# DRAM weight sums of a two-layer decoder step: first layer's along eight mixer units, second layer's along prompt attention

## The chip, the core and the metric

The program runs on one core of a Trainium2 chip. TensorE (PE) does the matmuls, VectorE (DVE), ScalarE (ACT) and GpSimd (POOL) the elementwise work, SyncE (SP) issues most transfers, and 16 DMA engines carry them. Each engine works through its own instructions in order and waits for others by semaphores. The metric is the device time of one launch in microseconds (us), the median of several runs. Float32 matmuls are made of three passes over operands that are split into a high and a low part ("h" and "l" in the names), so every weight tile that comes from DRAM is cast on ACT (high part) and subtracted on DVE or POOL (low part) before TensorE may use it.

## What is computed

One inference step of a decoder trunk with two layers, for a prompt of 1024 tokens and 8 x 8 sample tokens that share weights, width 1024, ConvGLU width 2816:

```python
mem_k_p, mem_v_p = memory_kv(mem_prompt, norm_mem, w_mem_kv)
# layer 0: mixer A, RWKV-7 time mix (12 heads of 64) beside memory attention (4 heads)
x = x + concat([o_tok, o_mem]) @ w_o[0]
x = x + conv_glu(rms_norm(x, norm_ffn[0]), state_conv[0], w_ffn_up[0], ...)
ckv, kpe = shared_latent(x, pos, ...)
# layer 1: mixer B, latent attention, 6 heads: causal for the prompt,
#          against 4096 cached tokens in pages for the samples
x = x + concat([o, o_mem]) @ w_o[1]
x = x + conv_glu(rms_norm(x, norm_ffn[1]), state_conv[1], w_ffn_up[1], ...)
y = rms_norm(x, final_norm)

def conv_glu(xn, conv_prev, w_up, conv_w, conv_b, w_down):
    u = xn @ w_up                       # (tokens, 2 * 2816): gate and val
    conv = causal_conv3(gate, conv_prev, conv_w, conv_b)
    return (silu(conv) * val) @ w_down, ...
```

The up product `xn @ w_up` is done by a Strassen-like scheme with seven products in place of eight. Some of the seven need sums of blocks of `w_up`; these sums don't depend on any activation.

## The kernel before

**The sums.** `sum_weights(l)` (L1284) makes four DRAM tensors for layer l, each 512 x 2816 in float32: `vg`, `gg`, `vgg` and `all`. It does so with DMAs alone. `move` (L1289) cuts one tensor into four transfers of 128 rows, 1408 KB each. A plain copy goes out on SP's queue, an accumulating add (`accum_op=ALU.add`) on POOL's. The source's order is: copy `vg`, copy `gg`, add to `vg`, add to `gg`, copy `vgg` from `vg`, add to `vgg`, copy `all` from `vgg`, add to `all`; four transfers each, so 32 a layer, 16 copies and 16 adds. A copy from a sum waits for the adds to it, an add for the copy before it, row block by row block. `load_up` (L1302) reads the four tensors in the ConvGLU of the same layer (the tiles `wa`); layer 0's ConvGLU begins some 1200 us after the start, layer 1's some 2700 us.

**Mixer A.** `mixer_a` (L273) runs 12 units, (half, head pair): units 0 to 5 for the first 512 prompt tokens, 6 to 11 for the rest and the samples. Three stages are woven together: the projections of unit i (`front`), the chunk-inner matrices of unit i-1 (`a_inner`) and the recurrent chain of unit i-2 (`chain`, which ends with the store `odp<-y`, L1060). Each `front` reads weight tiles of 128 x 4 x 128 (`wr<-in_w_in_a`, L207, three buffers) on SP's queue, casts them on ACT (`wh`, L210) and subtracts on POOL (`wl`, L211). `merge` takes steps from several generators by their weights; beside the first unit it takes the memory projection (`memory_kv`, loads `q<-in_w_mem_kv`), beside each later unit `sums`. `sums` is the sequence of both layers' sums, 64 steps, six a unit.

**Prompt attention.** `prompt_attention` (L1924) runs 24 units, (head, pair of query blocks), with scores of one unit beside the output of the unit before, and beside them `head_proj` (weights `w_q_b`, `w_kv_b`) and `val_proj` (weights `vr`) of the next heads. Each unit stores `odp<-ob` through two `ob` buffers. After every second head's rotary step POOL copies four small tiles (`qe<-lr`, L1787). The cached pages for the decode stage that follows are gathered on POOL's queue (`dc` and `dk`).

**What sets the order.** The code is traced in the order in which `merge` takes the steps. A scheduler then places every instruction on its engine's list by priority and by simulated readiness, so an instruction that waits for nothing can move far ahead of its place in the source. SP's and POOL's lists are the order of their DMA issues. `keep_in_program_order` ties an instruction behind the one traced just before it on the same engine.

Of the kernel before, what the change touches and what calls it, by code (L numbers as in the profile page):

```python
# [100 lines left out]
class Step:  # L101
# [171 lines left out]
    def mixer_a(s, od, qmd, kvd):  # L273
# [51 lines left out]
        def front(u):  # L325
            h, p = u
            if p == 0:
                yield from s.a_norm(h)
                yield from s.a_lora(h)
            if p == 2:  # L330
                yield from s.a_gate(h)
            ctx[u] = {}
            yield from s.a_front(p, h, ctx[u])

        def chain(u):
            h, p = u
            ctx[u]["y"] = s.t(ap, [128, 576], "y", 2)
            for g in s.groups(h):
                yield from s.a_chain(p, h, ctx[u], *g)
            yield from s.a_out(p, h, ctx.pop(u))  # L340
# [26 lines left out]
        s.mslot = (ap, "q", 512, s.QB)  # L367
        s.ended = False
        mkv = s.memory_kv(kvd, 0, ("tp", "ch", "y"))
        sums = s.seq(s.sum_weights(0), s.sum_weights(1))  # L370
        for i in range(nu):
            g = []
            if i == 1:
                for j in range(1, (len(s.prows) + 127) // 128):
                    s.load_params(j, [nc.sync])
            if i > 1:
                g.append((chain(units[i - 2]), s.PW[0] + s.PW[1] * units[i - 2][0], s.PW[2]))
            if i:
                u = units[i - 1]
                g.append((s.a_inner(u[1], u[0], ctx[u]), s.PW[3] + s.PW[4] * u[0], s.PW[5]))  # L380
            g.append((front(units[i]), 130 if units[i][1] else 220))
            if i == 0:
                g.append((mkv, 22))
            else:
                g.append((s.take(sums, 6), 6))
            s.merge(g)
        s.mslot = (ap, "xn", 584, 16)
        s.drain(last(s.seq(s.mem_attention(0, qmd, kvd, od, ("mm", "sm", "sm")), s.memory_kv(kvd, 1, ("sm", "mm", "mm")))))
# [895 lines left out]
    def sum_weights(s, l):  # L1284

        nc, W = s.nc, s.I["w_ffn_up"][l]
        S = s.wsum[l] = {z: s.t(s.dp, [512, DFF], f"ws{l}{z}", 1) for z in ("vg", "gg", "vgg", "all")}

        def move(z, src, **kw):  # L1289
            eng = nc.gpsimd if kw else nc.sync  # L1290
            for r in range(0, 512, 128):
                eng.dma_start(out=S[z][r:r + 128], in_=src[r:r + 128], **kw)
                yield

        def add(z, src):
            return move(z, src, accum_op=ALU.add, max_dma_last_dim=5632)

        g1, g2, v1, v2 = (W[r:r + 512, f:f + DFF] for f in (0, DFF) for r in (0, 512))
        yield from s.seq(move("vg", v1), move("gg", g1), add("vg", g1), add("gg", g2), move("vgg", S["vg"]),
                         add("vgg", g2), move("all", S["vgg"]), add("all", v2))  # L1300
# [623 lines left out]
    def prompt_attention(s, od):  # L1924
        s.AT = (3, 2, 1, 2, 6, 3)
        s.HN = ((8, 12, 12, 1000), (8, 12, 14, 1000))
        with s.phase("pa", dict(zip(("sc", "tp", "o", "mm"), s.AT))):
            s.hd = {h: {} for h in range(NH)}
            s.lay(*[([128, NP_], z, 2) for z in ("qs0", "qs1", "qnh", "qnl", "knh", "knl")],
                  ([128, 256], "vh", 8), ([128, 256], "vl", 8), ([128, 256], "ob", 2), ([128, 8], "sm", 4), ([128, 512], "P", s.AT[4]),  # L1930
                  ([128, 4, 256], "ptH", s.AT[5]), ([128, 4, 256], "ptL", s.AT[5]))
            s.qns = s.st([128, 6, 64], "qns", 1)
            s.drain(s.head_proj(0))
            us = [(h, Q, {}) for h in range(NH) for Q in (range(4) if h < NH - 1 else (3, 2, 1, 0))]
            pr = None
            for i in range(len(us) + 1):
                g = []
                ao = iter(())
                n = 0
                if i:  # L1940
                    h, Q, u = us[i - 1]
                    ao, n = s.attn_out(h, Q, u, od), 6 * Q + 6
                if i < len(us):
                    h, Q, u = us[i]
                    if Q == 0 and h % 2 == 0:
                        ao, n = s.seq(ao, s.val_proj(h)), n + 9
                    g.append((s.attn_scores(h, Q, u), 4 * Q + 8))
                    if Q == 0 and h + 1 < NH:
                        pr = s.head_proj(h + 1)
                    if pr is not None:  # L1950
                        k = s.HN[h % 2][Q]
                        g.append((s.take(pr, k), min(k, 40)))
                s.merge([(ao, n)] + g)


    def decode(s, od, side, xd):
# [466 lines left out]
```

## Time and profile before

| | us |
|---|---|
| median of 3 runs | 3606.49 (3594.25 to 3613.16) |
| the profiled run | 3604.49 |
| its span on the core | 3602.7 |
| TensorE busy | 3329.3 (92%) |
| VectorE busy | 2322.9 (64%) |
| ScalarE busy | 1722.7 (48%) |
| GpSimd busy | 806.1 (22%) |

The profile is one execution. Beside busy times it has the granted clock of TensorE as a share of 2.4 GHz (1.00 is the 2.4 GHz level, 0.50 the 1.2 GHz level, values between are a mix over the stretch), the busy share of the 16 DMA engines, and what each instruction waited for. A matmul at the lower level is busy for about twice the time, so busy TensorE is not the same as TensorE at its peak.

### The profile page before, as it was taken

How to read it: one execution, taken by the hardware profiler on the slowest of the kernel's cores; microseconds unless marked ns; L12 is line 12 of the kernel's file. 1: busy time of each engine (PE TensorE's matmuls, PEld its weight loads, DVE VectorE, ACT ScalarE, POOL GpSimd, SP SyncE). 2: the span in 40 equal slices, each digit the busy share in tenths (PEclk: the TensorE clock that was granted, in tenths of full speed). 3: DMA queues.
4: the chain of work that ended last, by engine and by line, in shares of the span. 5: the costliest groups of instructions: out<-in, count | busy, mean ns of one | idle time of the engine just before them, and what ended most of it. 6: DMA issues, size and time to landing. Idle time of an engine off the chain costs nothing. (4 is left out here: it accounts for less than half of the span.)

```text
span 3602.7 us, 68623 instructions
## 1 busy us (share of the span) xinstructions
PE 3329.3 (92%) x25782; PEld 2838.5 (79%) x25782; DVE 2322.9 (64%) x5353; ACT 1722.7 (48%) x3769; POOL 806.1 (22%) x1204
## 2 busy tenths in 40 slices
PE   6678789999996999999999899999999999999998
PEld 4444457777655999999999888855558999989998
DVE  4455466777653577778777547744445777787776
ACT  4333345555445454545454635533335644555444
POOL 4323213232101311113222400101102311132221
PEclk9877769999887999999999999999999999999999
DMA  7999931111314354445444310335424544545443
GB/s 223 266 246 249 242 93 39 34 44 46 93 34 164 90 164 142 144 135 160 138 141 124 93 57 30 113 111 178 150 82 120 155 141 132 145 130 148 134 141 112
DMA packets 608048, 466.90 MB, mean 130 GB/s; under 512 B 51546, under 2 KB 575598, under 8 KB 601060
## 3 DMA queue, kind: packets, MB, share of 16 engines
q1 hardware_dynamic: 583924, 359.80, 33.4%
q0 software_dynamic: 18848, 98.07, 10.7%
q10 hardware_dynamic: 4944, 4.65, 0.4%
q8 instruction: 202, 3.31, 0.4%
q14 instruction: 130, 1.06, 0.1%
HBM read 436.67 MB, written 118.03 MB: 154 GB/s over the span
## 5 line engine op out<-in xcount | busy, mean ns | idle before, releaser
L1354 PE MATMUL pmm<-xh,uh 128*128 128x272 f32 x2464 | 717.2, 291 | 5.1 <-ACT xh L1137 2.8
L1355 PE MATMUL pmm<-xl,uh 128*128 128x272 f32 x2464 | 714.0, 290 | 3.2 <-DVE xl L1138 2.9
L1356 PE MATMUL pmm<-xh,ul 128*128 128x272 f32 x2464 | 715.3, 291 | 0.4 <-DVE ul L1314 0.4
L1313 ACT CAST uh<-wa 128x512 fp32r<-128x512 f32 x610 | 378.4, 622 | 488.5 <-PE pmm L1355 306.5
L1314 DVE TENSOR_TENSOR ul<-wa,uh 128x512 fp32r<-128x512 f32 x610 | 435.5, 719 | 95.9 <-ACT uh L1313 59.6
L1354 PEld LDWEIGHTS pmm<-xh,uh 128*128 128x128 f32 x2464 | 466.8, 190 | 6.9 <-ACT xh L1137 4.3
L1355 PEld LDWEIGHTS pmm<-xl,uh 128*128 128x128 f32 x2464 | 467.8, 190 | 5.0 <-DVE xl L1138 4.5
L1356 PEld LDWEIGHTS pmm<-xh,ul 128*128 128x128 f32 x2464 | 466.7, 190 | 1.1 <-DVE ul L1314 0.9
L481 PE MATMUL pdn<-hh,wh 128*128 128x272 f32 x1248 | 360.9, 290 | 7.7 <-ACT hh L1137 3.9
L482 PE MATMUL pdn<-hl,wh 128*128 128x272 f32 x1248 | 358.4, 288 | 0.7 <-DVE hl L1138 0.7
L483 PE MATMUL pdn<-hh,wl 128*128 128x272 f32 x1248 | 357.2, 288 | 1.6 <-DVE wl L211 1.6
L210 ACT CAST wh<-wr 128x512 fp32r<-128x512 f32 (+2 forms) x363 | 200.5, 563 | 311.6 <-PE pdn L482 116.4
L1361 POOL TENSOR_TENSOR ext<-nt,nt 128x272 f32<-128x272 f32 (+2 forms) x132 | 119.0, 915 | 882.4 <-ACT uh L1313 721.4
L481 PEld LDWEIGHTS pdn<-hh,wh 128*128 128x128 f32 x1248 | 235.3, 189 | 12.9 <-ACT hh L1137 7.9
L483 PEld LDWEIGHTS pdn<-hh,wl 128*128 128x128 f32 x1248 | 235.0, 189 | 2.5 <-DVE wl L211 2.5
L482 PEld LDWEIGHTS pdn<-hl,wh 128*128 128x128 f32 x1248 | 235.2, 189 | 1.1 <-DVE hl L1138 1.1
L481 PE MATMUL pmm<-xn,wh 128*128 128x292 f32 (+2 forms) x552 | 214.6, 389 | 21.3 <-ACT wh L210 17.5
L1166 DVE TENSOR_TENSOR x<-x,pdn 128x272 f32<-128x272 f32 x288 | 125.4, 435 | 132.8 <-PE pdn L483 132.2
L483 PE MATMUL pmm<-xn,wl 128*128 128x292 f32 (+2 forms) x552 | 204.2, 371 | 1.6 <-POOL wl L211 1.4
L482 PE MATMUL pmm<-xn,wh 128*128 128x292 f32 (+2 forms) x552 | 204.9, 371 | 0.0
L211 DVE TENSOR_TENSOR wl<-wr,wh 128x512 fp32r<-128x512 f32 (+2 forms) x271 | 166.6, 624 | 47.5 <-ACT wh L210 43.7
L211 POOL TENSOR_TENSOR wl<-wr,wh 128x512 fp32r<-128x512 f32 (+1 forms) x92 | 118.3, 1289 | 238.6 <-ACT wh L210 214.0
(760 smaller groups left out, 7850.1 us busy)
## 6 DMA issues: line engine op xcount, KB each, us to landing
wa<-in_w_ffn_up SPq DMA_DIRECT2D x262, 256.0 KB
wr<-in_w_ffn_down SPq DMA_DIRECT2D x164, 256.0 KB
wr<-in_w_in_a SPq DMA_DIRECT2D x84, 256.0 KB
wr<-in_w_o SPq DMA_DIRECT2D x64, 256.0 KB
wa<-ws0vg SPq DMA_DIRECT2D x44, 256.0 KB
wa<-ws0all SPq DMA_DIRECT2D x44, 256.0 KB
wa<-ws1vg SPq DMA_DIRECT2D x44, 256.0 KB
wa<-ws1all SPq DMA_DIRECT2D x44, 256.0 KB
```

What stands on the lines that cost most here:

```text
L210: nc.scalar.copy(wh[:, :n, :m], wr[:, :n, :m])
L211: s.wl_eng.tensor_tensor(wl[:, :n, :m], wr[:, :n, :m], wh[:, :n, :m].bitcast(F32), ALU.subtract)
L481: nc.tensor.matmul(ps[:m, :n], wh[:, :m], xh[:, c0:c0 + n], start=(k == 0), stop=False)
L482: nc.tensor.matmul(ps[:m, :n], wh[:, :m], xl[:, c0:c0 + n], start=False, stop=False)
L483: nc.tensor.matmul(ps[:m, :n], wl[:, :m], xh[:, c0:c0 + n], start=False, stop=(k == last))
L1166: nc.vector.tensor_tensor(xv, xv, p[:, :n], ALU.add)
L1313: nc.scalar.copy(wh, w)
L1314: nc.vector.tensor_tensor(wl, w, wh.bitcast(F32), ALU.subtract)
L1354: nc.tensor.matmul(p, wh, xh[:, k], start=k == 0, stop=False)
L1355: nc.tensor.matmul(p, wh, xl[:, k], start=False, stop=False)
L1356: nc.tensor.matmul(p, wl, xh[:, k], start=False, stop=k == 3)
L1361: add = lambda eng, o, a, b, op=ALU.add: eng.tensor_tensor(o, a, b, op)
```

## The change

- In `mixer_a`, `sums` is now the first layer's 32 steps alone, and four steps are taken a unit, so that they spread over units 1 to 8.
- In `prompt_attention`, the second layer's 32 steps are taken, two a unit, beside the 25 rounds of its loop.
- In `move`, each DMA is tied behind the instruction traced before it on its engine.

The transfers are the same 64 with the same sizes and dependencies.

```diff
 def mixer_a(s, od, qmd, kvd):
...
-        sums = s.seq(s.sum_weights(0), s.sum_weights(1))
+        sums = s.sum_weights(0)
...
-                g.append((s.take(sums, 6), 6))
+                g.append((s.take(sums, 4), 4))
...
         def move(z, src, **kw):
             eng = nc.gpsimd if kw else nc.sync
             for r in range(0, 512, 128):
-                eng.dma_start(out=S[z][r:r + 128], in_=src[r:r + 128], **kw)
+                s.tc.keep_in_program_order(eng.dma_start(out=S[z][r:r + 128], in_=src[r:r + 128], **kw))
                 yield
...
 def prompt_attention(s, od):
...
             pr = None
+            sums = s.sum_weights(1)
             for i in range(len(us) + 1):
...
-                s.merge([(ao, n)] + g)
+                s.merge([(ao, n), (s.take(sums, 2), 2)] + g)
```

**First place, POOL's list in the mixer**, around the small copy `y_501` of one pair's inner stage. Names are tiles; L1292 is the DMA of `move`, L211 the low part of a weight tile. Before:

```order
L852 MEMSET q_1602 64x64
L853 MEMSET q_1602 64x64
L494 MEMSET ext_2088 128x1
L772 COPY y_501_2237<-c_eye_31_142 128x128
L760 TENSOR_TENSOR t_348_1432<-q_1431,c_tmask_138 64x256
L710 TENSOR_SCALAR bv_1569<-bv_1569,ptile_20_120 128x512
L1292 DMA ws0all_754<-in_w_ffn_up 128x2x1408
L211 TENSOR_TENSOR wl_2001<-wr_1998,wh_2000 128x512
```

Now:

```order
L760 TENSOR_TENSOR t_348_1430<-q_1428,c_tmask_138 64x256
L772 COPY y_501_2232<-c_eye_31_142 128x128
L499 COPY carry_163<-ext_1468 128x1
L614 MEMSET wl_1960 64x128
L615 MEMSET wl_1960 64x128
L1292 DMA ws0vg_751<-in_w_ffn_up 128x2x1408
L211 TENSOR_TENSOR wl_1991<-wr_1988,wh_1990 128x512
```

Just behind `y_501` stood the first add to `all`, with twelve adds ahead of it; now it is the first add of all, to `vg`. On SP the eight copies of `vg` and `gg` stand about where they stood, those of `vgg` and `all` come after the first store `odp<-y`, and the 32 transfers of layer 1 are gone from both lists here. The last four copies to `all` now stand just ahead of unit 4's store on SP's list. The rest of the mixer's instructions are the same ones, with a changed order on every engine; from the end of the mixer on, TensorE's list is as before but for a few places in prompt attention.

**Second place, SP's list in prompt attention**, from the load of head 3's `w_kv_b` on (`wr` are weight tiles, `ob` the stored outputs). Before:

```order
L1833 DMA vr_26508<-in_w_kv_b 128x2x128 x2
L207 DMA wr_25691<-in_w_kv_b 128x2x128
L1921 DMA odp_63<-ob_24801 128x256
L207 DMA wr_25967<-in_w_q_b 128x2x64 x2
L1921 DMA odp_63<-ob_24874 128x256
L1921 DMA odp_63<-ob_24993 128x256
```

Now:

```order
L1292 DMA ws1vgg_24547<-ws1vg_24545 32x11264 x2
L207 DMA wr_25678<-in_w_kv_b 128x2x128
L1921 DMA odp_63<-ob_24773 128x256
L1292 DMA ws1gg_24546<-in_w_ffn_up 128x2816
L207 DMA wr_25960<-in_w_q_b 128x2x64
L1921 DMA odp_63<-ob_24847 128x256
L1292 DMA ws1gg_24546<-in_w_ffn_up 128x2816 x3
L1921 DMA odp_63<-ob_24969 128x256
L207 DMA wr_25960<-in_w_q_b 128x2x64
L1833 DMA vr_26508<-in_w_kv_b 128x2x128 x2
```

Copies of 1408 KB, up to three in a row, now stand between the loads and stores; the first two `vgg` copies wait for adds.

**Third place, POOL's list at the end of prompt attention** (`qe<-lr` are the last pair's small copies, `dc` and `dk` the gathers for the decode stage). Before:

```order
L1787 COPY qe_4712_23552<-lr_25974 64x8x8
L1787 COPY qe_4713_23553<-lr_25974 64x8x8
L1976 DMA dc_27326<-in_cache_ckv,ix_23567 128x2048
L1977 DMA dk_27327<-in_cache_kpe,ix_23567 128x512
L1976 DMA dc_27330<-in_cache_ckv,ix_23567 128x2048
```

Now:

```order
L1787 COPY qe_4708_23516<-lr_25967 64x8x8
L1787 COPY qe_4709_23517<-lr_25967 64x8x8
L1292 DMA ws1all_24548<-in_w_ffn_up 128x2x1408 x4
L1977 DMA dc_27326<-in_cache_ckv,ix_23531 128x2048
L1978 DMA dk_27327<-in_cache_kpe,ix_23531 128x512
```

The last four adds stand between those copies and the gathers. Ahead of this, three adds to `vg` follow the first pair's `qe` copies, and the other nine (`vg` one, `gg` four, `vgg` four) stand between the second pair's and the last pair's.

## Rows read from the trace of the kernel before

**Rows 1.** The page's 40 slices: granted clock, and busy tenths of the DMA engines.

```profile
PEclk9877769999887999999999999999999999999999
DMA  7999931111314354445444310335424544545443
```

**Rows 2.** Busy time by stretch (start:end, length, engines), then clock, DMA share, GB/s.

```profile
40.00:455.00 415.00, 306.71 (x2150) 196.87 (x2149) 205.25 (x546) 155.98 (x335) 130.07 (x175) 0.77 0.98 253
455.00:516.00 61.00, 52.55 (x475) 34.02 (x477) 35.36 (x133) 27.96 (x78) 11.54 (x19) 0.63 0.40 113
516.00:615.00 99.00, 92.08 (x772) 73.15 (x772) 62.79 (x195) 50.98 (x121) 25.30 (x33) 0.83 0.13 34
615.00:930.00 315.00, 305.57 (x3016) 228.62 (x3015) 236.82 (x757) 160.86 (x402) 93.14 (x152) 0.96 0.17 43
930.00:1100.00 170.00, 147.50 (x1423) 91.72 (x1422) 90.03 (x301) 81.28 (x243) 12.10 (x31) 0.86 0.24 70
2135.00:2315.00 180.00, 176.84 (x1128) 153.94 (x1127) 137.48 (x397) 98.03 (x268) 2.79 (x12) 0.99 0.11 33
```

**Rows 3.** Line L1292's DMA issues: engine, tile, count, ns min/median/max, first to last start.

```profile
L1292 SPq DMA_DIRECT2D ws0vg<-in_w_ffn_up x4: 506/531/1057, 38.7 to 71.6; - x4
L1292 POOL DMA_DIRECT2D ws1all<-in_w_ffn_up x4: 1145/1153/1211, 411.4 to 463.3; - x4
```

**Rows 4.** DMA queues from 40 to 455 us (packets, MB, share), issues with us to landing.

```profile
q0 software_dynamic: 8432, 44.70, 55.9%
q1 hardware_dynamic: 30194, 60.05, 41.7%
...
wr<-in_w_in_a SPq DMA_DIRECT2D x36, 256.0 KB
ws0vg<-in_w_ffn_up POOLq DMA_DIRECT2D x4, 1408.0 KB, 15.7
...
ws1gg<-in_w_ffn_up POOLq DMA_DIRECT2D x4, 1408.0 KB, 20.9
```

**Rows 5.** Waits of ACT from 40 to 455 us: total us, times, longest.

```profile
ACT wh L210 <- DMA wr<-in_w_in_a: 89.5, 13, 13.3
```

**Rows 6.** Waits of PE from 40 to 455 us.

```profile
PE pch L2179 <- ACT q L1137: 25.9, 5, 10.7
PE py L949 <- ACT q L918: 23.6, 6, 12.0
PE pmm L481 <- ACT wh L210: 17.5, 4, 9.6
PE pch L917 <- ACT r L913: 13.2, 2, 9.4
```

**Rows 7.** Waits of PE from 615 to 930 us, the same chain instruction.

```profile
PE py L949 <- ACT q L918: 1.1, 3, 0.5
```

**Rows 8.** Busy time by stretch, two stretches of 12 us in the mixer.

```profile
384.00:396.00 12.00, 8.96 (x43) 6.00 (x44) 5.38 (x17) 5.97 (x16) 3.00 (x3) 0.50 1.09 403
504.00:516.00 12.00, 12.00 (x99) 7.81 (x102) 6.05 (x15) 7.79 (x14) 2.50 (x5) 0.50 0.00 1
```

**Rows 9.** POOL's timeline in prompt attention: start us, us, line, operation.

```profile
2146.18 1.05 POOL L1787 COPY qe<-lr 64x64 f32<-64x64 f32 x4 [33.91 <-DVE lr L1762]
2197.54 1.06 POOL L1787 COPY qe<-lr 64x64 f32<-64x64 f32 x4 [50.31 <-DVE lr L1762]
2271.34 1.07 POOL L1787 COPY qe<-lr 64x64 f32<-64x64 f32 x4 [72.75 <-DVE lr L1762]
2315.46 1.09 POOL L1976 DMA_INDIRECT dc<-in_cache_ckv,ix  x1 [43.04 <-PE pmm L483]
```

**Rows 10.** Timelines of SP and ACT: a load of `vr` and the cast that uses it.

```profile
2151.57 0.88 SPq L1833 DMA_DIRECT2D vr<-in_w_kv_b  x2
...
2162.42 0.64 ACT L1137 CAST vwh<-vr 128x512 fp32r<-128x512 f32 x1
```

**Rows 11.** Line L2039, decode's transposes of the gathered pages: first and last start.

```profile
L2039 PE MATMUL ptp<-ident,dc x128: 272/273/476, 2371.5 to 2449.3; 128*128 128x128 f32 x128
```

## The prediction

> **What bounds the kernel now.** The page's slices come first [rows 1]: the DMA engines are full in the first five slices of 90 us, and those are the slices where TensorE's clock falls to 0.7. From the fourteenth slice on the clock is full and nothing is to be had there from weight traffic. Stage by stage [rows 2]: from 40 to 455 us TensorE is busy 306.71 of 415 us at a clock of 0.77, with DMA engines busy 0.98; from 615 to 930 us, the same kind of work with its other half of tokens, it is busy 305.57 of 315 us at 0.96, with DMA at 0.17. The first stretch is the sums' stretch: their first copy is issued at 38.7 us, their last add at 463.3 us [rows 3]. Both layers' 64 transfers lie in it.
>
> How a full DMA reaches TensorE is read from the waits. ACT stood 89.5 us, 13 times, waiting for a weight tile that it had to cast [rows 5]. ACT works in order, so what the recurrent chain needs from ACT stands behind the cast. TensorE's longest waits are on ACT: 25.9, 23.6, 17.5 and 13.2 us, 80.2 us in all [rows 6]. The second of them, the chain's `py` waiting for ACT's `q`, is up to 12.0 us long here and at most 0.5 us, 1.1 us in total, from 615 to 930 us [rows 7]. So 80 of the 108 us in which TensorE is not busy go back to ACT, most of it to late weights.
>
> **What one transfer costs the DMA engines.** From 40 to 455 us POOL's queue has 55.9% of the engines' time for 44.70 MB, which are 31 adds: 232 us, or 7.5 us each. SP's queue has 41.7% for 60.05 MB, 173 us; a copy of 1.44 MB has its share by bytes, 4.2 us [rows 4]. One layer's sums are thus 16 x 7.5 + 16 x 4.2 = 187 us of all 16 engines.
>
> **Part 1: the mixer loses the second layer's 32 transfers, and the first layer's 32 are spread.** POOL's list shows it: at `y_501` twelve adds had been issued, now none; only the eight copies of `vg` and `gg` keep their early place on SP. Until the first store `odp<-y` this leaves about a fifth of the sums' traffic; later units have four transfers of 4.2 to 7.5 us each. Over the stretch DMA should be about half busy. I take three quarters of the 80.2 us off the path: 60 us. The last quarter stays, since a weight tile that is issued just behind a copy still waits for it and for adds that share the engines. The bounds: 0, if other waits take the place, and 80.
>
> The clock is the second term. Work at full clock from 40 to 455 us is 306.71 x 0.77 = 236 us. With fewer gaps I take 0.86, which the mixer's tail has, where DMA is at 0.24 and the same small chain matmuls run [rows 2]: 236/0.86 = 275, so 32 us less. The bounds are 0 and, at the 0.96 of 615 to 930 us, 236/0.96 = 246, 61 us less. I take the middle value because two stretches pull apart [rows 8]: from 384 to 396 us, with DMA full, TensorE is busy 8.96 of 12 us, with gaps, and at 0.50, the 1.2 GHz level; but from 504 to 516 us it is busy for all of 12.00 us, DMA at 0.00, and is at 0.50 too. What it did there was small chain matmuls and transposes, and freed DMA won't change that. From 455 to 615 us I take nothing.
>
> The Trainium skill says in "TensorE: Matmul & The Clock Gate", section "HAM oscillation — how this bites in real kernels", that matmuls between waits for DMA run at the throttled clock, so that a gap costs twice. The row at 384 us agrees, the one at 504 us shows the lower level without such a wait. By that rule alone the gain would be the larger one that is the first rival below.
>
> **Part 2: prompt attention takes the second layer's 187 us of DMA.** From 2135 to 2315 us it has TensorE busy 176.84 of 180 us at 0.99 and DMA at 0.11 [rows 2], so there is room of 160 us and some more on either side. It needs 21 loads of 64 to 128 KB by the code (nine `w_q_b`, six `w_kv_b`, six `vr`), where the mixer's stretch has 36 of 256 KB [rows 4]. Of these most are issued well ahead; the pair of `vr` at 2151.57 us has 10.9 us until its cast at 2162.42 us [rows 10], and on SP the fourth `vg` copy (4.2 us) now stands ahead of it, with three adds in flight beside it, issued once the `qe` copies of 2146.18 us are done. That load and the two behind it may be late by 3 to 5 us each. Later, POOL's nine adds leave after 2197.54 us and need 9 x 7.5 = 68 us, with SP's loads between them; SP's copies to `all` wait for adds to `vgg`, and the `odp<-ob` stores behind them hold up ACT only when both buffers are taken. For all this I take 12 us, and 3 us for clock: 15 us. The bounds: 0, if all of it hides; and from above, loads that wait as in the mixer, 89.5/36 = 2.5 us each, 52 us for 21, with the clock at the mixer's 0.77 for a third of the stretch, 176.84 x 0.99 x (1/0.77 - 1/0.99)/3 = 17 us: 69 us.
>
> The Trainium skill's "DMA: Bandwidth & Descriptors", section "Issuing engines are not separate DMA queues", says that transfers of all engines run on the same 16 DMA engines and interleave. The 55.9% and 41.7% that add up to 98% agree. It speaks against the change: the same DMA time is moved, none is saved. If each us of the sums cost prompt attention what it costs TensorE in the mixer, 80.2/(31 x 7.5 + 31 x 4.2) = 0.22, it would be 41 us in place of 15.
>
> **Part 3: POOL and SP as queues.** In the mixer an add is now issued long after its copy, so POOL, with `wl` behind it, should wait less than before. In prompt attention POOL has nothing but the twelve `qe` copies; they come late by little, and the decode stage is their reader. The last four adds are issued after 2271.34 us, 4 x (7.5 + 4.2) = 47 us, so they end near 2325 us, and the gathers, first issued at 2315.46 us [rows 9], start about 10 us late. Decode's first transposes come at 2371.5 us [rows 11]: nothing, and 10 to 20 us if the chain of sums slips by 40 us. The layer-1 ConvGLU reads the sums hundreds of us later.
>
> **Part 4: the mixer's order** changes on all engines beyond the sums. The rows of before can't price that; I take 0 and 25 us to either side.
>
> **Sum.** The profiled run took 3604.5 us (span 3602.7), 2 us under the median 3606.5. Mixer stalls -60, clock -32, prompt attention +15, the rest 0: -77. 3604.5 - 77 = 3527.5, say **3528 us**.
>
> **The rivals.**
> *The clock comes back in full.* All 80 us of waits go; the clock is 0.96 from 40 to 615 us: -61 for the first stretch, and for the 160 us behind it 52.55 x 0.63 + 92.08 x 0.83 = 110 us of work, 110/0.96 = 114 against 145 busy, -31. With +15: 3604.5 - 172 + 15 = 3447 us. For it: at 615 us nothing but DMA and the other half of tokens differ. Against: the 0.50 at 504 us.
>
> *The first units are bound by their own chain.* Then ACT's waits are replaced by others and the clock stays: -40 of stalls, no clock, +15: 3580 us. For it: from 455 to 516 us, DMA already at 0.40, the work per us is 52.55 x 0.63/61 = 0.54, no better than 236/415 = 0.57 in the full stretch. Against: that is the change to the second half of tokens, with its norm and transposes and no projections to fill.
>
> *Prompt attention is held up by the chain of sums (slower).* SP waits in order at the eight copies to `vgg` and `all` for adds that took 15.7 to 20.9 us to land [rows 4]: 8 x 17 = 136 us of SP, with the next head's weights and the `odp<-ob` stores behind. If all of it reaches TensorE, 3604.5 - 92 + 136 = 3648 us. It makes the kernel slower from the point where more than 92 of the 136 us get through. Against: adds and copies stand tens of us apart on the lists, and most loads are early.
>
> *It doesn't do what it says.* The lists are not strictly the source's: on POOL one add to `gg` stands ahead of two to `vg`, and the eight copies of `vg` and `gg` stay in the fullest part. If those first 165 us are what costs, the mixer gains 25 us at most, prompt attention takes 15 to 25 back: 3600 us.
>
> **How the numbers follow.** Forecast (3495 to 3565) 0.53; clock in full (3440 to 3495) 0.15; chain bound (3565 to 3590) 0.16; no effect, near 3600, 0.08; slower by prompt attention 0.08. The range holds the first three but for the far part of the second: 3455 to 3590 us. About 0.5%, 18 us, is what a measurement of this kernel can tell from no change; the faster side, below 3588 us, has 0.82, within 0.5% 0.10, slower 0.08.
>
> **What would show it.** Right: from 40 to 455 us DMA near half, ACT's wait for `wr<-in_w_in_a` under 30 us, TensorE's waits on ACT under 25 us, a clock of 0.82 or more, and the first store `odp<-y` some tens of us earlier; in prompt attention DMA near full with TensorE still over 95% busy at 0.95 or more. Wrong: ACT's waits gone and the stretch no shorter (the chain bounds it), or `odp<-ob` stores and `wh` casts in prompt attention that wait tens of us for DMA.

## The result

The changed kernel takes 3550.38 us (median of 4 runs, 3542.77 to 3551.58) against 3607.12 us: a ratio of 0.9843, 95% interval 0.9813 to 0.9873. Forecast were 3528 us, from 3455 to 3590: the direction and the range are right, the point is 22 us too fast. The profiled run of the changed kernel took 3542.8 us, the fastest of its four, 61.7 us less than that of before. Three marks in the two traces say where they went:

| stretch | before, us | after, us | difference |
|---|---|---|---|
| start to the first `qe` copy (prompt attention begins) | 2146.2 | 2012.0 | -134 |
| first `qe` copy to decode's first transposes | 225.3 | 293.3 | +68 |
| from there to the end | 1231.2 | 1235.7 | +4 |

Half of what the mixer gained was paid back in prompt attention.

The page of the changed kernel, slices as in [rows 1]: the DMA engines are no longer full in the first five slices, and slices 24 and 25 (2036 to 2213 us, in prompt attention) are now the fullest; there the clock has fallen to 0.8.

```profile
PEclk9998599998889999999999988999999999999999
DMA  6464444123244554364432589345423544545443
```

The windows of [rows 2], in the changed kernel; the first and the last row are new, and so are the two of before in the second block. All columns are as there.

```profile
40.00:331.00 291.00, 258.77 (x2145) 169.96 (x2146) 207.85 (x542) 153.99 (x331) 105.44 (x150) 0.95 0.54 142
40.00:455.00 415.00, 369.30 (x3089) 253.05 (x3089) 287.86 (x828) 215.81 (x491) 134.29 (x190) 0.87 0.53 138
...
615.00:930.00 315.00, 298.08 (x2973) 208.28 (x2970) 220.15 (x711) 160.70 (x436) 67.16 (x117) 0.95 0.21 58
...
2012.00:2305.00 293.00, 228.70 (x1387) 194.38 (x1385) 170.28 (x498) 122.21 (x338) 32.73 (x40) 0.87 0.72 187
```

```profile
40.00:453.00 413.00, 304.71 (x2141) 195.60 (x2139) 203.86 (x543) 155.06 (x331) 128.07 (x174) 0.77 0.98 253
2146.00:2371.00 225.00, 214.23 (x1386) 183.38 (x1386) 169.31 (x499) 121.86 (x338) 14.39 (x24) 0.99 0.18 64
```

Two pairs of rows hold the same work, as their matmul counts show. **The mixer up to its third store `odp<-y`** (2141 and 2145 matmuls) ended at 453 us and ends at 331: 122 us less. TensorE's idle time fell from 108.3 to 32.2 us (-76), its busy time from 304.7 to 258.8 us (-46), with the clock at 0.95 for 0.77. By the twelfth and last store the gain is 138 us, so nearly all of it comes in these first units. **Prompt attention** (1386 and 1387 matmuls) went the other way: idle from 10.8 to 64.3 us (+53.5), busy from 214.2 to 228.7 us (+14.5), the clock at 0.87 for 0.99.

The twelve stores `odp<-y`, before and changed (last: start of the first and of the twelfth):

```profile
L1060 SPq DMA_DIRECT2D odp<-y x12: 326/351/3653, 297.3 to 1095.5; - x12
L1060 SPq DMA_DIRECT2D odp<-y x12: 327/342/1382, 209.9 to 957.7; - x12
```

Waits of the changed kernel in the mixer, 40 to 455 us (us in total, times, longest), the answers to [rows 5, 6]:

```profile
ACT wh L210 <- DMA wr<-in_w_in_a: 13.8, 2, 12.0
PE pch L917 <- ACT r L913: 10.9, 3, 10.4
...
PE py L949 <- ACT q L918: 2.4, 8, 0.3
```

Late weights cost ACT 13.8 us there in place of 89.5. In prompt attention, 2012 to 2306 us, they now appear:

```profile
PE psc L1865 <- ACT P L1883: 23.5, 7, 15.9
...
ACT wh L210 <- DMA wr<-in_w_o: 18.2, 1, 18.2
ACT wh L210 <- DMA wr<-in_w_q_b: 16.4, 1, 16.4
...
PE pmm L481 <- ACT ql L1823: 15.2, 1, 15.2
PE po L1915 <- ACT ptH L1137: 14.0, 10, 10.8
...
ACT wh L210 <- DMA wr<-in_w_kv_b: 12.2, 1, 12.2
...
ACT ob L1920 <- DMA odp<-ob: 7.2, 1, 7.2
```

Three late loads and one store hold ACT for 18.2 + 16.4 + 12.2 + 7.2 = 54.0 us, and TensorE, whose longest waits are again on ACT, is idle 53.5 us more. (That the two sums agree so closely is no proof by itself; e3 below is.) The transfers come in bursts. Line L1292 in the changed kernel (columns as in [rows 3]):

```profile
L1292 SPq DMA_DIRECT2D ws1gg<-in_w_ffn_up x4: 501/545/596, 2049.2 to 2056.4; - x4
L1292 POOL DMA_DIRECT2D ws1gg<-in_w_ffn_up x4: 1584/2283/2979, 2079.0 to 2081.1; - x4
L1292 POOL DMA_DIRECT2D ws1vgg<-in_w_ffn_up x4: 1135/1820/2529, 2127.6 to 2129.7; - x4
```

Two per round are written; but a place in a list sets no time. These four copies wait for nothing, and the adds only for their copies, so the four copies start within 7 us of each other and four adds within 2 us. What holds SP in this stage are the copies that read a sum, 46.6 us in all (2000 to 2320 us):

```profile
SPq L1292 <- DMA ws1vg<-in_w_ffn_up: 27.0, 3, 12.9
...
SPq L1292 <- DMA ws1vgg<-in_w_ffn_up: 19.6, 1, 19.6
```

### The profile page after: what moved, and what is told of

It is laid out like the page before. It is cut to its first block, busy times and chain, and to the rows that moved or that the text cites. A ratio compares the mean times of both kernels' runs of the same rounds, so it can differ in the third digit from the quotient of the medians.

```text
span 3541.0 us, 68611 instructions
## 1 busy us (share of the span) xinstructions
PE 3283.3 (93%) x25782; PEld 2815.4 (80%) x25782; DVE 2331.1 (66%) x5353; ACT 1724.7 (49%) x3769; POOL 811.9 (23%) x1204
## 3 DMA queue, kind: packets, MB, share of 16 engines
q0 software_dynamic: 18848, 98.07, 10.9%
## 5 line engine op out<-in xcount | busy, mean ns | idle before, releaser
L211 DVE TENSOR_TENSOR wl<-wr,wh 128x512 fp32r<-128x512 f32 (+2 forms) x271 | 166.6, 624 | 91.4 <-ACT wh L210 87.5
L481 PE MATMUL pmm<-xn,wh 128*128 128x292 f32 (+2 forms) x552 | 206.5, 374 | 2.6 <-DVE e L511 1.9
L482 PE MATMUL pmm<-xn,wh 128*128 128x292 f32 (+2 forms) x552 | 194.8, 353 | 0.0
L483 PE MATMUL pmm<-xn,wl 128*128 128x292 f32 (+2 forms) x552 | 194.4, 353 | 0.0
L211 POOL TENSOR_TENSOR wl<-wr,wh 128x512 fp32r<-128x512 f32 (+1 forms) x92 | 119.6, 1304 | 197.7 <-ACT wh L210 151.5
```

Source lines behind the costliest of these rows:

```text
L211: s.wl_eng.tensor_tensor(wl[:, :n, :m], wr[:, :n, :m], wh[:, :n, :m].bitcast(F32), ALU.subtract)
L481: nc.tensor.matmul(ps[:m, :n], wh[:, :m], xh[:, c0:c0 + n], start=(k == 0), stop=False)
L482: nc.tensor.matmul(ps[:m, :n], wh[:, :m], xl[:, c0:c0 + n], start=False, stop=False)
L483: nc.tensor.matmul(ps[:m, :n], wl[:, :m], xh[:, c0:c0 + n], start=False, stop=(k == last))
```

## Experiments

Each ratio is against the kernel before on the same chip, with its 95% interval. "Start" is the first `qe` copy, "stretch" the time from it to decode's first transposes, both from one trace.

| kernel | median, us | ratio (interval) | start | stretch |
|---|---|---|---|---|
| before | 3607 to 3613 | 1 | 2146 | 225 |
| changed | 3550.4 | 0.9843 (0.9813 to 0.9873) | 2012 | 293 |
| e1: tie alone | 3556.5 | 0.9861 (0.9831 to 0.9892) | 2080 | 235 |
| e2: places alone | 3605.1 | 0.9990 (0.9973 to 1.0008) | 2133 | 234 |
| e3: no layer 1 sums | 3492.7 | 0.9670 (0.9644 to 0.9696) | 2022 | 234 |
| e4: no layer 0 sums | 3529.8 | 0.9773 (0.9743 to 0.9802) | 2005 | 291 |
| e5: layer 1 along ConvGLU | 3516.7 | 0.9741 (0.9705 to 0.9777) | 2044 | 232 |
| e6: copies on GpSimd | 3582.0 | 0.9917 (0.9881 to 0.9953) | 2018 | 329 |
| e7: e5, three a unit | 3535.5 | 0.9802 (0.9761 to 0.9842) | 2065 | 232 |
| e8: e5, even spread | 3495.2 | 0.9676 (0.9630 to 0.9721) | 2025 | 234 |
| e9: one a round | 3526.2 | 0.9763 (0.9724 to 0.9802) | 2018 | 269 |
| e10: `w_o` casts late | 3547.9 | 0.9826 (0.9787 to 0.9864) | 2034 | 277 |
| e11: e8, six a unit | 3537.7 | 0.9800 (0.9752 to 0.9849) | 2072 | 235 |

### Which part of the change does it: e1 and e2

e1 is the kernel before with the tie alone; e2 is the changed kernel without the tie:

```diff
-                eng.dma_start(out=S[z][r:r + 128], in_=src[r:r + 128], **kw)
+                s.tc.keep_in_program_order(eng.dma_start(out=S[z][r:r + 128], in_=src[r:r + 128], **kw))
```

> The kernel before with one edit: every sum DMA is tied to its place in the source; both layers' 64 transfers stay along the mixer, six a unit over units 1 to 11. Theory (crowding: what costs is 64 transfers within 455 us, and prompt attention pays 66 to 68 us for its 32): the mixer is nearly as fast as in the changed kernel (start of prompt attention 110 to 134 us earlier than before), prompt attention as before, 3475 to 3500 us. Rival (the mixer gains only because the second layer's transfers leave it): under half of that gain, 3540 us or more.

> The changed kernel without the tie: the sums are taken where the change takes them (first layer along eight mixer units, second layer along prompt attention), but the scheduler may move them. On the lists all 64 then stand in the first five units again. Theory: the tie does the work, so this is within 15 us of the kernel before, 3595 to 3615 us. Rival (the place in the source matters by itself): 3550 us, as the changed kernel.

In e2 all 64 transfers are back in the first units, whatever the source says (last add at 450.8 us), ACT's wait is back (line L1292's last row, then ACT's wait from 40 to 455 us), and the time is that of before:

```profile
L1292 POOL DMA_DIRECT2D ws1all<-in_w_ffn_up x4: 1147/1166/1195, 407.3 to 450.8; - x4
```

```profile
ACT wh L210 <- DMA wr<-in_w_in_a: 89.0, 13, 13.8
```

In e1 the 64 transfers run along the whole mixer. Its windows show both halves paying a little:

```profile
40.00:455.00 415.00, 359.17 (x2947) 243.11 (x2945) 279.04 (x810) 209.71 (x480) 136.31 (x188) 0.85 0.66 173
455.00:930.00 475.00, 436.34 (x4083) 317.78 (x4082) 306.29 (x960) 216.24 (x539) 135.11 (x209) 0.88 0.54 135
```

So the tie alone gives the changed kernel's gain; the intervals of the two overlap for the most part. The changed kernel starts prompt attention another 68 us earlier than e1 (2080 to 2012) and takes 58 us longer over it (235 to 293): nothing measurable is left of the rest of the change. That rest is two things, layer 1's transfers out of the mixer and four a unit in place of six; e11 below takes them apart. My expectation for e1, a time below 3500 us, was wrong: the numbers are the rival's, 3540 us or more and just under half of the mixer's gain (66 of 134 us).

### What the transfers cost: e3 and e4

e3 leaves layer 1's sums out (its ConvGLU reads plain weight blocks), e4 layer 0's, in `sum_weights`:

```diff
+        if l == 1:
+            s.wsum[l] = {z: W[0:512, 0:DFF] for z in ("vg", "gg", "vgg", "all")}
+            return
```

> The changed kernel without the second layer's sums: its ConvGLU reads plain weight blocks in their place (same loads), so that layer's product is another one. Theory (the 32 transfers cost prompt attention 66 to 68 us): 3475 to 3490 us, and no wait of ACT for a weight tile of over 3 us in prompt attention. Rival (prompt attention is slower because of its changed instruction order): no faster than the changed kernel, 3540 to 3552 us.

> The changed kernel without the first layer's sums: its ConvGLU reads plain weight blocks in their place (same loads). Theory (four transfers a unit are nearly hidden): 0 to 15 us faster than the changed kernel, 3535 to 3550 us. Rival (a quarter or more of the old stalls remains in the mixer): 25 us faster or more, 3525 us or less.

Without layer 1's 32 transfers prompt attention is short again, with its full clock (e3):

```profile
2022.00:2255.00 233.00, 216.89 (x1384) 184.71 (x1382) 169.12 (x499) 121.95 (x338) 14.42 (x24) 0.98 0.18 62
```

They are what it pays for: 293 - 234 = 59 us, 1.9 us each, and no weight tile is late there any more; the time, 3492.7 us, is just above the theory's range. Layer 0's cost 3550.4 - 3529.8 = 21 us by the medians, between the two expectations; the two traces show less, 3542.8 - 3534.2 = 9 us, of which 5 lie before the twelfth store (957.7 and 953.1 us). With no transfer in it, then, the mixer is hardly shorter than with four a unit. The stretch is 6 to 10 us longer than before in every kernel without transfers in it, also in e2, which has no tie: some 9 of the 68 us belong neither to the transfers nor to the tie, and their cause stays open.

### SP's wait or the DMA engines: e6

SP stood 46.6 us in prompt attention before copies that wait for adds, with weight loads behind it. e6 takes the copies off SP:

```diff
-            eng = nc.gpsimd if kw else nc.sync
+            eng = nc.gpsimd if kw or l else nc.sync
```

> The changed kernel with layer 1's 16 copies issued by GpSimd, as its 16 adds are, so that SyncE's list holds no copy that waits for an add. Theory SP (prompt attention loses its time because SyncE stands before a copy that waits for an add, with the next weight loads behind it): the 46 us of SyncE's waits on ws1vg and ws1vgg go, first qe copy to first gather falls from 227 us to 185 us or less, and the time is 3500 to 3520 us. Theory engines (the copies and adds take the 16 DMA engines from the weight loads, whoever issues them): that stretch stays at 215 us or more, ACT still waits for late weights, and the time is 3540 to 3560 us.

SP no longer waits for any add, and the loads are as late as ever:

```profile
ACT ob L1920 <- DMA odp<-ob: 31.6, 2, 21.4
...
ACT wh L210 <- DMA wr<-in_w_q_b: 22.4, 2, 11.9
ACT wh L210 <- DMA wr<-in_w_o: 19.1, 1, 19.1
...
ACT wh L210 <- DMA wr<-in_w_kv_b: 16.8, 1, 16.8
```

SP's wait for the adds is not what makes them late; they are late when POOL issues all the sums, too. The Trainium skill, "DMA: Bandwidth & Descriptors", section "Issuing engines are not separate DMA queues", says that transfers interleave on the same 16 engines whoever starts them; these rows agree. That e6 is slower than the changed kernel by some 30 us was in neither expectation: the four rows add up to 89.9 us of ACT, 36 more than the 54.0 above, and the stretch is 36 us longer. Four `vg` copies that left before the stretch now lie in it; whether that is all of it stays open.

### Fewer at a time: e9

e9 issues layer 1's first eight copies along the first ConvGLU, and the other 24 at one a round.

```diff
-                s.merge([(ao, n), (s.take(sums, 2), 2)] + g)
+                s.merge([(ao, n), (s.take(s.sums, 1), 1)] + g)
```

> Layer 1's first 8 transfers (copies that wait for nothing) along the first ConvGLU, the other 24 in prompt attention at one a round instead of two. Theory (what prompt attention loses is set by how full the DMA engines are when a weight load comes): half the rate leaves room between the bursts, first qe copy to first gather is 195 us or less (168 without sums, 227 with two a round), time 3505 to 3525 us. Rival (so much for each byte): 24 of 32 transfers cost 24/32 of 58 us, that stretch is 205 us or more, time 3530 to 3545 us.

The first gather was a bad mark: it stood on POOL behind adds that waited for copies.

```profile
2218.22 2.30 POOL L1292 DMA_DIRECT2D ws1all<-in_w_ffn_up  x2 [40.52 <-DMA ws1all<-ws1vgg]
...
2249.64 1.09 POOL L1980 DMA_INDIRECT dc<-in_cache_ckv,ix  x1 [0.31 <-ACT ob L1924]
```

By decode's transposes the stretch is 269 us: 36 us over e3 for 24 transfers, 1.5 us each in place of 1.9. Late loads of three weights still hold ACT for 18.1, 10.5 and 10.4 us. Half the rate makes each a fifth cheaper and does not hide them: nearer to "so much for each byte" than to "room between bursts", with the time between the two expectations.

### One late load less: e10

The scheduler had put two casts of `w_o`, read 450 us later, on ACT's list in prompt attention; one stood there 18.2 us. e10 holds those casts at their place in the source.

```diff
-            nc.scalar.copy(wh[:, :n, :m], wr[:, :n, :m])
+            keep(nc.scalar.copy(wh[:, :n, :m], wr[:, :n, :m]))
```

> The changed kernel with the ScalarE casts of layer 1's output projection weight held at their place in the source, behind decode; the changed kernel's scheduler put the first two of them on ScalarE's list in prompt attention, and one of them stood 18.2 us before its late load. Theory (every late load that ScalarE's list meets costs its own wait, and this one was avoidable): that wait goes, first qe copy to the first decode transposes falls from 293 us to 270 to 280 us, time 3528 to 3540 us. Rival (the DMA engines are full there, so the time moves to the next late load): the stretch stays at 285 us or more, time 3545 to 3556 us.

The wait on `w_o` is gone, the other two are unchanged (16.4 and 12.5 us), and the stretch is 16 us shorter, 277 us: ACT's in-order list does turn a late load that nobody needs yet into lost time. The median, 3547.9 us, does not show it, for two reasons that the trace has. Behind decode, where `w_o` is read, the held casts now wait for it (2600 to 2860 us; in the changed kernel this wait is 1.8 us), and from decode's transposes to the end it takes 1246.6 us in place of 1235.7, 11 of the 16 us back:

```profile
ACT wh L210 <- DMA wr<-in_w_o: 13.8, 6, 2.8
```

And the mixer's twelfth store came at 981 us, where it came at 958 to 970 in six others with the same placement of the sums there; why is not known (the profiled run is the slowest of its four). The stretch agrees with the theory, the time with the rival.

### A stage that can hide them: e5 and e8

e5 issues layer 1's transfers along layer 0's ConvGLU, one per chunk for 32 chunks. Nothing of them is left in prompt attention.

```diff
                 yield from up(h, c, operands[h], hs[h, i])
+                yield from s.take(sums, 1)
...
+        sums = iter(()) if l else s.sum_weights(1)
```

e8 spreads them evenly over its 44 chunks:

```diff
-                yield from s.take(sums, 1)
+                k = 32 * (22 * h + c)
+                yield from s.take(sums, (k + 32) // 44 - k // 44)
```

> The changed kernel with layer 1's 32 transfers taken out of prompt attention and issued one per chunk along the first layer's ConvGLU instead. Theory (a stage whose PE has work ahead and whose DMA is about half busy can hide them): prompt attention takes again the 168 to 169 us that it took without these transfers (first qe copy to first gather), the ConvGLU of the first layer is not longer by over 10 us, and the time is 3490 to 3510 us. Rival (each transfer costs some 1.8 us wherever it runs beside loads that PE needs, 58 us for 32): prompt attention is short, the ConvGLU is 40 us or more longer, and the time is 3535 to 3555 us.

> As the kernel that issues layer 1's 32 transfers along the first ConvGLU, but spread evenly over all its 44 chunks instead of one in each of the first 32. Theory (what they cost there is set by how full the DMA engines get: PE lost its time at 1400 to 1600 us, right after a slice with DMA at 0.98): the DMA share stays under 0.75 in every 100 us from 1200 on, ACT waits less for wa, and the time is 3492 to 3508 us. Rival (so much for each byte moved, or another place in the ConvGLU): 3510 to 3522 us, as with the first 32 chunks.

Two windows of the ConvGLU in the changed kernel, e5 and e8, in that order:

```profile
1300.00:1400.00 100.00, 99.54 (x790) 99.11 (x789) 77.57 (x137) 50.76 (x90) 16.32 (x26) 1.00 0.50 144
1400.00:1600.00 200.00, 193.47 (x1500) 190.35 (x1499) 158.50 (x291) 100.56 (x192) 51.45 (x79) 0.99 0.50 144
```

```profile
1300.00:1400.00 100.00, 99.78 (x794) 99.56 (x793) 73.95 (x129) 49.18 (x86) 22.16 (x30) 1.00 0.98 231
1400.00:1600.00 200.00, 176.20 (x1308) 170.54 (x1307) 144.11 (x268) 92.15 (x181) 49.76 (x73) 0.96 0.78 217
```

```profile
1300.00:1400.00 100.00, 99.55 (x790) 99.11 (x789) 78.42 (x136) 52.42 (x91) 22.90 (x32) 1.00 0.75 186
1400.00:1600.00 200.00, 191.52 (x1470) 188.09 (x1469) 152.86 (x284) 97.54 (x188) 51.98 (x76) 0.98 0.77 209
```

e5 came out between its two expectations. The DMA engines fill up from 1300 to 1400 us and TensorE loses 17 us behind that; over the whole ConvGLU ACT waits 25.6 us for `wa`. From the twelfth store to the first `qe` copy it takes 1079 us, against 1052 in e3. In e8 DMA has no such peak (it went to 0.81, above the 0.75 that I expected, without harm), the same stretch takes 1062 us, and the time, 3495 us, is that of e3, which leaves these sums out. The first ConvGLU hides them almost wholly: 10 us over e3 for 32 transfers, 0.3 us each. Its `w_ffn_up` tiles stand in eight `wa` buffers, where prompt attention has three `wr`, so that a load can be issued further ahead; that this is the reason is argued, not shown, since the two stages differ in much else. **e8 is faster than both kernels**: 0.9676 (0.9630 to 0.9721), some 55 us under the changed one. Against e5 the intervals still overlap a little.

### How fast in the mixer: e7 and e11

Layer 0's transfers at three a unit over eleven units (e7, on e5) and at six (e11, on e8), in place of four over eight.

```diff
-                g.append((s.take(sums, 4), 4))
+                g.append((s.take(sums, 3), 3))
```

> The kernel with layer 1's transfers along the first ConvGLU, and in the mixer three of layer 0's transfers a unit over eleven units instead of four over eight. Theory (what layer 0's transfers still cost, 21 us, is set by how full the DMA engines are at each moment): 5 to 15 us faster than the kernel with four a unit. Rival (it is so much for each transfer): the same within 4 us.

> Layer 1's transfers evenly along the first ConvGLU, as in the fastest run so far, and layer 0's 32 at six a unit instead of four. Theory (the mixer's loss goes with how full the DMA engines are): DMA above 0.70 in 40 to 300 us, ACT waits for wr again, 3505 to 3525 us. Rival (three a unit was slower than four because the transfers reached the later units, which stand them worse; so earlier is better): 3480 to 3492 us.

Both are slower, by 19 and 43 us. For six a unit the theory had that, and DMA above 0.70 came too (0.71 from 40 to 300 us). But the wait that it named did not come back: in those 260 us ACT waits for weights no longer than in e8 (e8 first, then e11), and the time is above its range.

```profile
ACT wh L210 <- DMA wr<-in_w_in_a: 12.4, 2, 10.6
ACT wh L210 <- DMA wr<-in_w_in_a: 13.2, 2, 7.8
```

What differs is the clock (0.87 from 40 to 220 us, against 0.95 in e8) and the stores: the third comes 15 us later than in e8, the sixth 24, the twelfth 44. The last add of e11 leaves at 426 us, so 20 of the 44 us are lost behind the sixth store (575 us), where none of its transfers run. Three a unit goes against both expectations. So DMA's fullness is not the whole price in the mixer: each placement also changes what all engines do next to what. How much that is, by itself, stays open.

e11 differs from e1 in one thing, where layer 1's transfers run: along the ConvGLU in place of the mixer. First and twelfth store of e8, e11 and e1:

```profile
L1060 SPq DMA_DIRECT2D odp<-y x12: 326/342/498, 213.3 to 963.2; - x12
L1060 SPq DMA_DIRECT2D odp<-y x12: 327/348/506, 224.3 to 1007.0; - x12
L1060 SPq DMA_DIRECT2D odp<-y x12: 327/345/497, 219.7 to 1028.2; - x12
```

The changed kernel's twelfth store came at 957.7 us. So of the 70 us by which e1 is behind it, 49 come with six a unit and 21 with layer 1's 32 transfers, 0.7 us each: spread along the mixer they cost about a third of what they cost in prompt attention. This rests on one trace of each kernel.

## Why the prediction was right, and where it was not

**What bounds it: right for the mixer.** Late weights on ACT's list and the gaps that they leave in TensorE's work were the loss; e2 brings back wait and time together. That the clock fell through those gaps is read from the rows and not shown by itself: e11 lost clock with ACT's wait unchanged. The announced signs came in the mixer: DMA near half (0.53), ACT's wait under 30 us (13.8), TensorE's waits on ACT short (10.9 and 2.4 us in the rows above), a clock over 0.82 (0.87), the first store 87 us earlier. In prompt attention they did not: TensorE was busy 78% at 0.87, not over 95% at 0.95, and the sign of being wrong was there, casts that wait for DMA (12 to 18 us each, 47 in all).

**Part 1, stalls -60, clock -32: both too small.** On equal work they are -76, near the bound of 80, and -46, halfway from 32 to the bound of 61, and 12 us more came behind the third store. I kept a quarter of the waits for loads issued just behind a copy; measured, ACT kept 13.8 of 89.5 us.

**The clock: the middle value was too low, its reason held.** I had capped the clock because of the stretch at 504 us, at the 1.2 GHz level with no DMA at all. The slices say the same and I read past it: the lowest clock of before, 0.6, is in the sixth slice, where DMA is at 0.3, not in the full ones. Nearly the same work lies at 378 to 418 us in the changed kernel, and is at that level there too (before first, then after):

```profile
500.00:516.00 16.00, 16.00 (x237) 10.37 (x238) 8.77 (x21) 9.29 (x18) 3.16 (x6) 0.50 0.01 3
516.00:540.00 24.00, 21.41 (x116) 14.50 (x117) 16.46 (x73) 11.21 (x36) 1.10 (x3) 0.50 0.07 23
```

```profile
378.00:394.00 16.00, 14.65 (x216) 9.55 (x210) 10.66 (x25) 9.97 (x21) 4.19 (x5) 0.50 1.00 186
394.00:418.00 24.00, 21.21 (x118) 14.61 (x118) 15.61 (x74) 11.41 (x35) 0.37 (x2) 0.50 0.09 26
```

It stands just behind the work that I costed, though, not within it. So the work up to the third store came to 0.95, and the rival of the full clock over all 575 us failed at this place. The Trainium skill's rule on gaps ("TensorE: Matmul & The Clock Gate", section "HAM oscillation — how this bites in real kernels") fits the first units, where gaps and low clock went together, and again does not account for the fully busy 500 to 516 us.

**Part 2, prompt attention +15: the step that failed.** It measured +68, 53.5 of idle time and 14.5 of busy time at a lower clock; 59 of it are the transfers' (e3). My upper bound was 69, from the mixer's 2.5 us per load and its clock; that row of the mixer was the right one to take, and I set it aside for the room that a DMA share of 0.11 seemed to leave. An average share is not room for a load that is needed within some 10 us, when a burst of adds at 7.5 us each is in front. The load that I named, `vr`, was not among the late ones; `w_q_b`, `w_kv_b` and the early `w_o` were. The 41 us, from what each us of the sums cost TensorE in the mixer, were nearer than my 15.

**Part 3, queues 0: nearly so.** Decode starts 66.0 us behind the first gather, 56 before, and the rest of the program is 4 us longer. **Part 4, the mixer's order, 0 within 25:** the 12 us above lie inside it.

**The rivals.** The slower one had the right place and the wrong road: prompt attention was held up, but not by SP's 46.6 us of waits (e6), and 68 us instead of 136. The chain-bound one falls with the third store, 122 us earlier once ACT's waits were gone. The one in which the change doesn't do what it says falls with e1 and e2: the tie does what it says, and without it the places in the source change nothing. That the two errors, -42 in the mixer and +53 in prompt attention, nearly cancel is why the sum came out within 15 us of the profiled run's -61.7: that nearness was luck.

## What to carry to other kernels

A stage in which the DMA engines are idle on average need not have room for background traffic: prompt attention with DMA at 0.11 paid 1.9 us for each 1.44 MB transfer, the ConvGLU with DMA at 0.5 some 0.3 us. What may tell them apart is how many tiles ahead the weights of the running stage are loaded; that was not tested by itself. Spread the traffic evenly, since in the ConvGLU a peak near full was followed by lost TensorE time (e5), and look at the lists or at the trace for where it really is issued: a place in the source moved nothing here without a tie, and a tie fixes the order, not the time. Where an in-order engine casts weights, look as well for casts that the scheduler has put early: one late load for later work holds up everything now. Holding them back is not free either: in e10 the casts then waited where they were needed.

## What the runs showed of the hardware

One accumulating DRAM-to-DRAM add of 1408 KB took POOL 1.12 to 1.32 us to issue in the mixer (before, changed, e8) and in the ConvGLU (e8). In the bursts of prompt attention single records last up to 2.98 us (`ws1gg` above), but they overlap: four together take 5.05 us, 1.26 us each.

```profile
2079.03 5.05 POOL L1292 DMA_DIRECT2D ws1gg<-in_w_ffn_up  x4
```

And a low TensorE clock went with more than one thing in one kernel: beside gaps behind late weights, a stretch of small chain matmuls and transposes was at the 1.2 GHz level with DMA at 0.01 and at 1.00 alike.
